# Splitting the attention output weights on GpSimd, and the last token tile in column pieces

## The chip, the cores and the metric

The kernel runs on one core of a Trainium2 chip. The metric is device microseconds of one execution, the median of several runs. A core has a matmul engine (TensorE, PE in the views, with its weight loads shown apart as PEld), an engine for elementwise work on two inputs (VectorE, DVE), one for functions of one input (ScalarE, ACT), a general engine (GpSimd, POOL) and a queue that issues transfers (SyncE, SP).

## The reference

One layer of a diffusion backbone: 1024 latent tokens and 256 context tokens, 1024 features, everything in float32.

```python
h_x = _modulate(x, g_pre_mix[l], sh1, sc1)
u_x, q_x, k_x, v_x = _project(h_x, w_in[l])
attn_x = _neighbourhood_attention(q_x, k_x, v_x, k_c, v_c, rpb[l])   # 8 heads of 64, 8 x 16 window + context keys
mix_x = jnp.concatenate([_pool_mixer(u_x, ...), attn_x], axis=-1) @ w_out[l]
x = x + gt1 * _rmsnorm(mix_x, g_post_mix[l])
y_x = _sq_relu_mlp(_modulate(x, g_pre_mlp[l], sh2, sc2), w_mlp_in[l], w_mlp_out[l])   # 1024 -> 4096 -> 1024
x = x + gt2 * _rmsnorm(y_x, g_post_mlp[l])
```

The change touches two places: the preparation of `w_out` while the attention runs, and the end of the second MLP matmul with the last norm and the residual sum.

## The kernel before

A float32 operand of a large matmul is written as a sum of two parts, `hi` (the value rounded to the matmul's short float32 format, type `F32R`) and `lo` (what is left). A product is then three matmuls: hi by hi, hi by lo, lo by hi (`three`, lines 167 to 170). So each weight tile has to be split once before use: a rounding copy for `hi` and a subtraction of two tiles in SBUF for `lo`.

**Attention** (lines 641 to 854). The work is cut into 32 units: 4 pairs of heads by 8 bands of 128 tokens. A loop over `i` runs as a pipeline written out by hand: for unit `i` the scores (`scores`, PE matmuls `S`, line 669, then one DVE instruction per head that adds a bias table and takes the minimum, line 683), the exponentials (`exps`, ACT, line 692); for unit `i - 1` the reciprocals of the sums (`share`, DVE: `RECIPROCAL` line 696, then a `COPY` that spreads them over 128 columns, `rb`, line 698); for unit `i - 2` the transposes (`turn`, PE, line 711: first `rb`, into `pa` and `pz`, then the probabilities, into `T`) and the copies of their results (lines 725 and 730); for unit `i - 3` the products with the values (`values`, PE, `pa`, line 745), and for unit `i - 4` the weighting (`weighed`, DVE, line 755). PE, ACT, DVE and SP keep the order of the program in this loop (`in_order`); GpSimd does not, there a planner in the compiler sets the order.

Two kinds of side work lie in the loop. After each group of 8 units the group's result is split for the output projection (`mixed_split`, a copy on ACT, line 766, and a subtraction on DVE, line 767, 128x512 each, named `mix`). And the first 512 output columns of `w_out`, four tiles `raw_o[0, kk]` of 128x1024 that are loaded at `i` in `LOADS`, are split in eight halves of 128x512, at `i` in `HALVES`: again a copy on ACT (`wo_..h`, line 766) and a subtraction on DVE (`wo_..l`, line 767). GpSimd meanwhile only makes the bias tables (`tables`, line 613, 12 instructions of 128x128 for each pair of heads). The first matmuls that use the split weights come after the scores of the last unit (`out_sums`, `po`).

**The end** (lines 1212 to 1321). The second MLP matmul is computed in a scheme of seven block products P1 to P7, each for four token tiles `t` of 128 tokens and 512 columns. The last products are P3 into `z` (upper 512 columns of tiles 0 to 3) and P4 into `v` (lower 512 columns of tiles 4 to 7, after P7 and the first half of P4 were summed there). For each tile the last sums are 12 matmuls (`z`) or 24 (`v`) of 128x512, and then `finish` runs:

- `c`, DVE, line 1263: the PSUM result plus `u2`, 128x512;
- the residual of the tile before (`end`: `xo`, DVE, line 1255, then its store on SP's queue, line 1256);
- `gated`: the mean square of `c` (ACT, line 130, tile `jy`, with an instruction that reads out the accumulator) and `row`, `c` times the gate (DVE, line 1246);
- `vy` (DVE, line 137) adds the mean squares of the two halves, and `ry` (GpSimd, line 139) takes the power -1/2.

Tile 7 is the last one. Its residual is done in two pieces of 512 columns, each followed by its store.

Of the kernel before, what the change touches and what calls it, by code (L numbers as in the profile page):

```python
# [10 lines left out]
F32 = mybir.dt.float32  # L11
F32R = mybir.dt.float32r
# [5 lines left out]
P = 128  # L18
D = 1024
# [60 lines left out]
def hybrid_block(ctx, tc, x, ctx_in, w_mod, b_mod, gp1, gp2, w_in, pool_w, rpb, w_out, w1, w2, vectors,  # L80
                 mask, edge, out):
    nc = tc.nc
    sub, mul, add = ALU.subtract, ALU.mult, ALU.add
# [3 lines left out]
    whl = ctx.enter_context(tc.tile_pool(name="whl", bufs=8))  # L87
# [7 lines left out]
    def sm(name, n, bufs=1):  # L95
        return small.tile([P, n], F32, tag=name.split("_")[0], name=name, bufs=bufs)
# [5 lines left out]
    @contextmanager  # L102
    def in_order(*engines):
        block = nc.cur_bb
        n = len(block.bb.instructions)
        last = {}
        yield last
        assert nc.cur_bb is block
        for i in block.bb.instructions[n:]:
            if i.engine in engines:  # L110
                if i.engine in last:
                    tc.add_manual_dep(i, last[i.engine].name,
                                      mybir.DependencyInfo(mybir.DependencyClass.NoSync, mybir.DependencyReason.DATA),
                                      reason="order")
                last[i.engine] = i
# [13 lines left out]
    def mean_square(junk, src, ms):  # L129
        nc.scalar.activation(junk, src, AF.Square, scale=D ** -0.5, accum_out=ms)  # L130

    def rsqrt_of(name, ms, more=None):
        v = sm(f"v{name}", 1, 4)
        if more is None:
            nc.vector.tensor_scalar_add(v, ms, EPS)
        else:
            nc.vector.scalar_tensor_tensor(v, ms, EPS, more, add, add)  # L137
        r = sm(f"r{name}", 1, 4)
        nc.gpsimd.tensor_tensor(r, v, nhalf, ALU.pow)  # L139
        return r  # L140
# [26 lines left out]
    def three(ps, ahi, alo, bhi, blo, first, last, more=False):  # L167
        nc.tensor.matmul(ps, ahi, bhi, start=first, stop=False, skip_group_check=more)  # L168
        nc.tensor.matmul(ps, ahi, blo, start=False, stop=False, skip_group_check=more)  # L169
        nc.tensor.matmul(ps, alo, bhi, start=False, stop=last, skip_group_check=more)  # L170
# [46 lines left out]
    def lasting(name):  # L217
        return ps_t.tile([P, 512], F32, tag="T", name=name)
# [4 lines left out]
    with tc.tile_pool(name="ps1", bufs=6, space=PSUM) as ps1, tc.tile_pool(name="tmp1", bufs=3) as tmp:  # L223

        def bank(name):
            if name[:2] == "pm" or name in ("pxt0_6", "pxt0_7", "pxt1_6", "pxt1_7", "pct2", "pct3"):
                return lasting(name)
            return ps1.tile([P, 512], F32, tag="mm", name=name)
# [7 lines left out]
        last = startup.enter_context(in_order(ET.PE, ET.Activation, ET.DVE, ET.SP))  # L236
# [192 lines left out]
        for k in range(KT):  # L429
            for i in range(2):  # L430
                o = (k % 2) * 256 + i * P
                nc.tensor.transpose(pct[k // 2][:, o : o + P], cp[i][:, k * P : (k + 1) * P], ident)
        hc = []
        for k in range(KT):
            if k % 2 == 0:
                hp = page(f"hc{k}", F32R)
            o = (k % 2) * 512
# [9 lines left out]
        rest, closing = [], []  # L447
# [49 lines left out]
        for i in range(2):  # L497
            ps = bank(f"pkc{i}")
# [8 lines left out]
        for i in range(2):  # L507
            ps = bank(f"pvc{i}")
# [11 lines left out]
        for m in range(NM):  # L520
            ps = bank(f"pv{m}")
# [59 lines left out]
        for g in range(4):  # L581
            up = page(f"u{g}")
            for b in range(2):
                ps = bank(f"pu{g}_{b}")
# [56 lines left out]
    with (  # L641
# [4 lines left out]
        bank = lasting  # L646
# [112 lines left out]

        kks = (2, 3, 0, 1)  # L760
        raw_o, wo = {}, {}
        LOADS, HALVES = (8, 10, 17, 19), (12, 13, 14, 20, 21, 22, 28, 30)
        lows = []

        def high(src, hi, lo):
            nc.scalar.copy(hi, src)
            lows.append(lambda: nc.vector.tensor_tensor(lo, src, hi.bitcast(F32), sub))
# [6 lines left out]
            mp = mix[b][4 + j] = page(f"mix{b}_{4 + j}", F32R)  # L774
            high(mixed[j, b], mp[:, :512], mp[:, 512:])

        def weight_split(n):
            kk, cs = kks[n // 2], slice(n % 2 * 512, n % 2 * 512 + 512)
            if n % 2 == 0:
                wo[kk] = [whl.tile([P, 1024], F32R, tag="hl", name=f"wo0_{kk}{x}") for x in "hl"]  # L780
            hi, lo = wo[kk]
            high(raw_o[0, kk][:, cs], hi[:, cs], lo[:, cs])

        def weight_load(h, kk):
            raw_o[h, kk] = page(f"wor{h}_{kk}")
# [21 lines left out]
        with in_order(ET.PE, ET.Activation, ET.DVE, ET.SP):  # L807
            queries(1, 1, bank("pq1_1"), 0)
            for i in range(N + 4):
                if i < N and units[i][1] == 2 and units[i][0] < 3:  # L810
                    tables(units[i][0] + 1)
                if i in LOADS:
                    weight_load(0, kks[LOADS.index(i)])
                if i == N - 2:
                    G1 = gate_page("a")
                if i > 3:
                    weighed(i - 4)
                low()
                if i > 8 and i % 8 == 7:
                    mixed_split(i // 8 - 1, 1)  # L820
                if i > 0 and i % 8 == 0:
                    mixed_split(i // 8 - 1, 0)
                if i in HALVES:
                    weight_split(HALVES.index(i))
                if i < N:
                    scores(i)
                else:

                    if i == N:
                        po = ps_s.tile([P, 1024], F32, tag="S", name="po")[:, :512]  # L830
                    out_sums(po, wo, 0, ((0, 1), (2, 3, 4), (5, 6, 7), ())[i - N])
                if 1 < i <= N + 1:
                    turn(i - 2)
                    fifth_kept(i - 2)
                if i < N:
                    exps(i, 0)
                if 1 < i <= N + 1:
                    turn_kept(i - 2, 0, nc.scalar.copy)
                if i < N:
                    exps(i, 1)  # L840
                if 1 < i <= N + 1:
                    turn_kept(i - 2, 1, nc.vector.tensor_copy)
                if i < 2:
                    queries(2 + i, 1, bank(f"pq{2 + i}_1"), 0)
                if 0 < i <= N:
                    share(i - 1)
                if 2 < i <= N + 2:
                    values(i - 3)
            mixed_split(3, 1)
            low()  # L850
            out_kept(0, 0, po, page("jo0_0")[:, :512])
            po = bank("po1")
            out_sums(po, wo, 1, range(8))
            out_kept(0, 1, po, page("jo0_1")[:, :512])

    with tc.tile_pool(name="ps2", bufs=6, space=PSUM) as ps2:
# [6 lines left out]
      with ExitStack() as tmp2:  # L863
        tmp = tmp2.enter_context(tc.tile_pool(name="tmp2", bufs=4))
# [74 lines left out]
        for t in out_group(1, range(NT)):  # L939
            rs = rsqrt_of(f"m_{t}", ssm[0][:, t : t + 1], ssm[1][:, t : t + 1])  # L940
            xt = page(f"xr{t}")
# [16 lines left out]
        NG = NPAIR // 2  # L958
# [218 lines left out]
        made = {}  # L1177
# [29 lines left out]
        with tc.issue_after(first[ET.PE]), in_order(ET.PE, ET.Activation, ET.DVE, ET.SP):  # L1207
# [5 lines left out]
            tmp = tmp2.enter_context(tc.tile_pool(name="tmp3", bufs=4))  # L1213
# [5 lines left out]
                both = [page(f"{name}{i}") for i in range(2)]  # L1219
                return [both[t // 2][:, (t % 2) * 512 : (t % 2) * 512 + 512] for t in range(4)]  # L1220

            def token_sums(ps, t, groups, first, last, more):
                n = 2 * len(groups)
                for j in range(n):
                    a, w = groups[j // 2]
                    o = (j % 2) * 512
                    three(ps[t], a[0][:, o + t * P : o + (t + 1) * P], a[1][:, o + t * P : o + (t + 1) * P],
                          w[0][:, o : o + 512], w[1][:, o : o + 512], first and j == 0, last and j == n - 1, more=more)

            def group(ps, name, g, more=False):  # L1230
                prepare()
# [5 lines left out]
            sq = [sm(f"sy{h}", NT) for h in range(2)]  # L1237
            rows = {}
# [10 lines left out]
            ending = []  # L1249

            def end():
                for m, rs, xt, cuts in ending:
                    for c in range(cuts):
                        cs = slice(c * D // cuts, (c + 1) * D // cuts)
                        nc.vector.scalar_tensor_tensor(xt[:, cs], rows[m][:, cs], rs, xt[:, cs], mul, add)
                        nc.sync.dma_start(og[m][:, :, cs], xt[:, cs])
                ending.clear()

            def finish(m, h, src, xt, cuts):
                if m > 5:  # L1260
                    end()
                c = tmp.tile([P, 512], F32, tag="t", name=f"c{m}", bufs=3)
                nc.vector.tensor_tensor(c, src, u2[m % 4], add)
                end()
                gated(m, h, c)
                ending.append((m, rsqrt_of(f"y_{m}", sq[0][:, m : m + 1], sq[1][:, m : m + 1]), xt, cuts))

            x = four("pyx")
            for g in range(NG):
                group(x, "P1", g)  # L1270
                if g == 4:
                    G2 = gate_page("b")
# [4 lines left out]
            for g in range(NG):  # L1277
                group(y, "P6", g)
                if g == NG - 1:
                    u2 = halves("u2")  # L1280
# [6 lines left out]
            v, z = four("pyv"), four("pyz")  # L1287
# [10 lines left out]
            for g in range(NG // 2):  # L1298
                group(v, "P4", g, more=True)
                group(z, "P3", g, more=True)  # L1300
                c = half(4 + g, 1)
# [6 lines left out]
            xts = {}  # L1308
# [5 lines left out]
                nc.sync.dma_start(xts[m], x1d[m])  # L1314
            for t in range(4):
                token_sums(z, t, [made["P3", g] for g in (NG - 2, NG - 1)], False, True, True)
                finish(t, 1, z[t], xts[t], 1)
            for t in range(4):
                token_sums(v, t, [made["P4", g] for g in range(NG // 2, NG)], False, True, True)
                finish(4 + t, 0, v[t], xts[4 + t], 1 + (t == 3))  # L1320
            end()


# [28 lines left out]
```

## Time and profile before

| | us |
|---|---|
| median of 3 runs | 1063.97 (1063.96 to 1064.71) |
| the profiled execution | 1063.25 |
| its span, first to last instruction | 1061.5 |

| engine | busy us | share of the span | instructions |
|---|---|---|---|
| PE | 1045.0 | 98% | 5873 |
| DVE | 685.6 | 65% | 1072 |
| ACT | 506.8 | 48% | 881 |
| POOL | 55.7 | 5% | 109 |

Shares are means over stages with different limits, and consecutive matmuls overlap in the records, so a busy PE is not a PE at its peak. The chain of waits (the work that ended last, followed back from the end) tells which engine sets the time in which stage. The mean granted TensorE clock is 0.997. Views used: the page, the chain in stretches of time, the groups of instructions, single lines of the program with minimum, median and maximum of their durations, and the timeline.

### The profile page before, as it was taken

What the parts mean: (1) busy time and instruction counts of PE and PEld (TensorE: products, weight loads), DVE (VectorE), ACT (ScalarE), POOL (GpSimd) and SP (SyncE); (2) the same over time, 40 slices, a digit from 0 to 9 for tenths busy, and PEclk for the clock granted to TensorE, in tenths of its full rate; (3) what the DMA queues carried; (4) which work ended last, traced back from release to release, by engine and by line L of the source; (5) the groups of instructions that cost most, each with busy time, mean ns of one, the idle gap of its engine ahead of it and who ended that gap; (6) DMA issues with size and microseconds to landing.
All of it is one profiled execution on the core that took longest, in us unless ns stands there. A gap on an engine that the chain in (4) does not pass through costs nothing.

```text
span 1061.5 us, 15251 instructions
## 1 busy us (share of the span) xinstructions
PE 1045.0 (98%) x5873; PEld 856.4 (81%) x5873; DVE 685.6 (65%) x1072; ACT 506.8 (48%) x881; POOL 55.7 (5%) x109
## 2 busy tenths in 40 slices
PE   7999999999999999999999999999999999999996
PEld 6788888867888888888888888888888888888885
DVE  6436634855999235799986666665577566557586
ACT  7554121235998123876555455554553335334441
POOL 2020000040120002200000000000000000000001
PEclk9999999999999999999999999999999999999998
DMA  9905740441111605445845445345597666546556
GB/s 343 324 21 198 243 174 0 138 134 40 42 41 47 174 1 171 145 149 183 259 168 175 140 138 190 129 151 196 209 355 253 243 238 220 192 164 205 173 188 206
DMA packets 94268, 179.37 MB, mean 169 GB/s; under 512 B 6898, under 2 KB 39154, under 8 KB 94196
## 3 DMA queue, kind: packets, MB, share of 16 engines
q1 hardware_dynamic: 76644, 144.80, 41.6%
q10 hardware_dynamic: 16272, 29.40, 7.5%
q0 software_dynamic: 1280, 4.21, 1.1%
q8 instruction: 46, 0.75, 0.3%
q14 instruction: 26, 0.21, 0.1%
HBM read 140.62 MB, written 37.76 MB: 168 GB/s over the span
## 4 chain that ended last, share of the span: by engine, by line
PE 89%; ACT 3%; DVE 3%; DMA 2%; SPq 1%; issue 1%; POOL 1%; POOLq 0%; DVEq 0%; ACTq 0%
PE pk L382 4%; PE S L669 3%; PE pa L745 3%; PE pyv L169 3%; PE pyv L168 3%; PE pyz L169 3%; PE pyz L168 3%; PE pyx L169 3%; PE phv L170 3%; PE phz L170 3%; PE pyx L170 3%; PE phz L168 3%; PE phv L168 3%; PE phv L169 3%; PE phz L169 3%; PE pyx L168 3%
## 5 line engine op out<-in xcount | busy, mean ns | idle before, releaser
L1001 ACT ACTIVATE c<-c 128x512 f32<-128x512 f32 x48 | 30.3, 632 | 60.4 <-DVE c L1114 23.8
L692 ACT ACTIVATE sp<-sp,nm 128x640 f32<-128x640 f32 (+1 forms) x64 | 51.3, 802 | 8.4 <-DVE nm L683 7.8
L683 DVE CUSTOM_DVE_ANT_0 sp<-S,tab 128x640 f32<-128x640 f32 (+1 forms) x56 | 42.8, 802 | 16.5 <-PE S L669 9.4
L144 DVE TENSOR_TENSOR wpS<-S,wpS 128x512 fp32r<-128x512 f32 x64 | 43.6, 686 | 11.8 <-ACT wpS L143 11.8
L168 PE MATMUL phx<-thB,wpA 128*128 128x512 f32 x128 | 49.9, 390 | 0.0
L170 PE MATMUL phx<-thB,wpA 128*128 128x512 f32 x128 | 49.9, 390 | 0.0
L169 PE MATMUL phx<-tlB,wpA 128*128 128x512 f32 x128 | 49.8, 389 | 0.0
L143 ACT CAST wpS<-S 128x512 fp32r<-128x512 f32 x64 | 39.2, 616 | 17.9 <-PE phy L170 7.5
L139 POOL TENSOR_TENSOR ry<-vy,nhalf 128x1 f32<-128x1 f32 x8 | 4.4, 550 | 600.7 <-DVE vy L137 600.7
L1002 ACT ACTIVATE c<-c 128x512 f32<-128x512 f32 x48 | 30.3, 631 | 8.0 <-DVE sa L1072 7.4
L1108 DVE TENSOR_TENSOR c<-phz,u 128x512 f32<-128x512 f32 x16 | 11.1, 691 | 32.2 <-PE phz L170 32.1
L669 PE MATMUL S<-kT,q 64*128 64x384 f32 (+1 forms) x128 | 27.9, 495 | 0.4 <-DVE nm L683 0.4
L170 PEld LDWEIGHTS phx<-thB,wpA 128*128 128x128 f32 x128 | 24.0, 188 | 5.2 <-DVE wpA L144 0.2
L169 PEld LDWEIGHTS phx<-tlB,wpA 128*128 128x128 f32 x128 | 24.0, 188 | 5.0
L168 PEld LDWEIGHTS phx<-thB,wpA 128*128 128x128 f32 x128 | 24.0, 188 | 4.9
L805 DVE TENSOR_TENSOR mp<-pw,Ga 128x512 f32<-128x512 f32 x14 | 9.6, 688 | 27.5 <-ACT jo L130 27.5
L745 PE MATMUL pa<-pt,v 128*64 128x128 f32 x352 | 25.9, 279 | 1.0 <-ACT px L725 0.3
L168 PE MATMUL phy<-thT,wpS 128*128 128x512 f32 x64 | 24.9, 389 | 0.0
L169 PE MATMUL phy<-tlT,wpS 128*128 128x512 f32 x64 | 24.9, 389 | 0.0
L170 PE MATMUL phy<-thT,wpS 128*128 128x512 f32 x64 | 24.9, 389 | 0.0
L168 PE MATMUL phz<-thT,wpS 128*128 128x512 f32 x64 | 24.9, 389 | 0.0
L169 PE MATMUL phz<-tlT,wpS 128*128 128x512 f32 x64 | 24.9, 389 | 0.0
(924 smaller groups left out, 3267.5 us busy)
## 6 DMA issues: line engine op xcount, KB each, us to landing
b<-in_w SPq DMA_DIRECT2D x64, 512.0 KB, 4.6
hrS<-hdS SPq DMA_DIRECT2D x32, 512.0 KB, 4.7
hrA<-hdA SPq DMA_DIRECT2D x24, 512.0 KB, 5.2
wm<-in_w_mod SPq DMA_DIRECT2D x16, 512.0 KB, 9.6
wa_0w<-in_w SPq DMA_DIRECT2D x16, 512.0 KB, 5.2
wa_1w<-in_w SPq DMA_DIRECT2D x16, 512.0 KB, 4.1
hdA<-c ACTq DMA_DIRECT2D x32, 256.0 KB, 2.3
hdS<-sa ACTq DMA_DIRECT2D x32, 256.0 KB, 4.3
```

The source lines that it names most:

```text
L143: nc.scalar.copy(hi, src)
L144: nc.vector.tensor_tensor(lo, src, hi.bitcast(F32), sub)
L168: nc.tensor.matmul(ps, ahi, bhi, start=first, stop=False, skip_group_check=more)
L169: nc.tensor.matmul(ps, ahi, blo, start=False, stop=False, skip_group_check=more)
L170: nc.tensor.matmul(ps, alo, bhi, start=False, stop=last, skip_group_check=more)
L382: nc.tensor.matmul(pks[b][j], wk(wgt, k, low, j * P, P), r, start=(k == 0 and n == 0), stop=(k == KT - 1 and n == 2))
L669: nc.tensor.matmul(S[e][:, c0 : c0 + keys.shape[1]], q[hs, cols], keys[hs], start=True, stop=True)
L683: nc.vector.tensor_tensor_reduce(out=to, in0=s, in1=bt, scale=1.0, scalar=BIG, op0=add, op1=ALU.min, accum_out=nm)
L692: nc.scalar.activation(sp, sp, AF.Exp, bias=least[i, e], scale=-1.0, accum_out=sums[i][:, e : e + 1])
L745: nc.tensor.matmul(pa[e * HD : (e + 1) * HD, cols], v[:, f : f + HD], turns[i][:, e, c] if c < 4 else fifths[i][:, :, (e + 1) * HD : (e + ...
L1001: nc.scalar.activation(r, src, AF.Relu)
L1002: nc.scalar.activation(r, r, AF.Square)
```

## The change

First, `w_out`'s tiles are split by GpSimd, one whole 128x1024 tile at a time, at `i` = 11, 13, 21 and 23, with a copy and a subtraction, and ACT's and DVE's sixteen instructions for the halves are gone. `mixed_split` stays on ACT and DVE.

Second, tile 7's lower 512 columns are made in two pieces of 256. Before the last four tiles, `late` adds up the upper 256 of these columns as they stand in PSUM and `u2`, on DVE. Then 24 matmuls of 128x256 complete the first piece, 24 more compute the second piece's last part alone in another PSUM bank, and each piece has its own `c`, mean square and `row` (`finish_last`). One more small addition on DVE joins the mean squares. The residual and its store are done in three pieces, of 512, 256 and 256 columns.

```diff
-        LOADS, HALVES = (8, 10, 17, 19), (12, 13, 14, 20, 21, 22, 28, 30)
+        LOADS, SPLITS = (8, 10, 17, 19), (11, 13, 21, 23)
...
-        def weight_split(n):
-            kk, cs = kks[n // 2], slice(n % 2 * 512, n % 2 * 512 + 512)
-            if n % 2 == 0:
-                wo[kk] = [whl.tile([P, 1024], F32R, tag="hl", name=f"wo0_{kk}{x}") for x in "hl"]
-            hi, lo = wo[kk]
-            high(raw_o[0, kk][:, cs], hi[:, cs], lo[:, cs])
+        def weight_split(kk):
+            hi, lo = wo[kk] = [whl.tile([P, 1024], F32R, tag="hl", name=f"wo0_{kk}{x}") for x in "hl"]
+            nc.gpsimd.tensor_copy(hi, raw_o[0, kk])
+            nc.gpsimd.tensor_tensor(lo, raw_o[0, kk], hi.bitcast(F32), sub)
...
-                if i in HALVES:
-                    weight_split(HALVES.index(i))
+                if i in SPLITS:
+                    weight_split(kks[SPLITS.index(i)])
...
-            def token_sums(ps, t, groups, first, last, more):
+            def token_sums(ps, t, groups, first, last, more, c0=0, nc0=512):
...
+                    ws = slice(o + c0, o + c0 + nc0)
                     three(ps[t], a[0][:, o + t * P : o + (t + 1) * P], a[1][:, o + t * P : o + (t + 1) * P],
-                          w[0][:, o : o + 512], w[1][:, o : o + 512], first and j == 0, last and j == n - 1, more=more)
+                          w[0][:, ws], w[1][:, ws], first and j == 0, last and j == n - 1, more=more)
...
-                    for c in range(cuts):
-                        cs = slice(c * D // cuts, (c + 1) * D // cuts)
+                    for c0, c1 in zip(cuts, cuts[1:]):
+                        cs = slice(c0, c1)
...
+            def finish_last(m, pieces, xt):
+                end()
+                so = sm("so", 1)
+                for c0, src, more in pieces:
+                    cs = slice(c0, c0 + 256)
+                    c = tmp.tile([P, 512], F32, tag="t", name=f"c{m}_{c0}", bufs=3)[:, :256]
+                    nc.vector.tensor_tensor(c, src, more, add)
+                    jk = tmp.tile([P, 512], F32, tag="t", name=f"jy{m}_{c0}", bufs=3)[:, :256]
+                    s0 = sq[0][:, m : m + 1]
+                    mean_square(jk, c, s0 if c0 else so)
+                    nc.vector.tensor_tensor(rows[m][:, cs], c, G2[:, cs], mul)
+                    if c0 == 0:
+                        nc.vector.tensor_tensor(so, so, sq[1][:, m : m + 1], add)
+                ending.append((m, rsqrt_of(f"y_{m}", s0, so), xt, (0, 512, 768, 1024)))
...
-            for t in range(4):
-                token_sums(v, t, [made["P4", g] for g in range(NG // 2, NG)], False, True, True)
-                finish(4 + t, 0, v[t], xts[4 + t], 1 + (t == 3))
+            late = u2[3][:, 256:]
+            nc.vector.tensor_tensor(late, v[3][:, 256:], late, add)
+            groups = [made["P4", g] for g in range(NG // 2, NG)]
+            for t in range(3):
+                token_sums(v, t, groups, False, True, True)
+                finish(4 + t, 0, v[t], xts[4 + t])
+            v[3] = v[3][:, :256]
+            token_sums(v, 3, groups, False, True, True, 0, 256)
+            rest = {3: bank("pye_0")[:, :256]}
+            token_sums(rest, 3, groups, True, True, False, 256, 256)
+            finish_last(7, ((0, v[3], u2[3][:, :256]), (256, rest[3], late)), xts[7])
             end()
```

More of the change, by code (lines that the diff above doesn't have):

```diff
@@ L1257, in end, with finish @@
                 ending.clear()
-            def finish(m, h, src, xt, cuts):
+            def finish_last(m, pieces, xt):
[12 more added lines that the diff above has]
+                ending.append((m, rsqrt_of(f"y_{m}", s0, so), xt, (0, 512, 768, 1024)))
+            def finish(m, h, src, xt):
                 if m > 5:
@@ L1265, in finish @@
                 gated(m, h, c)
-                ending.append((m, rsqrt_of(f"y_{m}", sq[0][:, m : m + 1], sq[1][:, m : m + 1]), xt, cuts))
+                ending.append((m, rsqrt_of(f"y_{m}", sq[0][:, m : m + 1], sq[1][:, m : m + 1]), xt, (0, D)))
             x = four("pyx")
@@ L1316, in hybrid_block @@
                 token_sums(z, t, [made["P3", g] for g in (NG - 2, NG - 1)], False, True, True)
-                finish(t, 1, z[t], xts[t], 1)
-            for t in range(4):
-                token_sums(v, t, [made["P4", g] for g in range(NG // 2, NG)], False, True, True)
-                finish(4 + t, 0, v[t], xts[4 + t], 1 + (t == 3))
+                finish(t, 1, z[t], xts[t])
+            late = u2[3][:, 256:]
[9 more added lines that the diff above has]
+            finish_last(7, ((0, v[3], u2[3][:, :256]), (256, rest[3], late)), xts[7])
             end()
```

## The prediction

> **What bounds the kernel now.** I read the page first, for the engines' shares and the chain.
>
> ```profile
> span 1061.5 us, 15251 instructions
> PE 1045.0 (98%) x5873; PEld 856.4 (81%) x5873; DVE 685.6 (65%) x1072; ACT 506.8 (48%) x881; POOL 55.7 (5%) x109
> PE 89%; ACT 3%; DVE 3%; DMA 2%; SPq 1%; issue 1%; POOL 1%; POOLq 0%; DVEq 0%; ACTq 0%
> ```
>
> PE carries 89% of the chain, so taking work from ACT or DVE is worth only what those engines hold on the chain in that stage. GpSimd is nearly idle. Next, the chain in two stretches of the attention: an inner unit without a weight half, then units 11 and 12, then the other places where a weight half lies on the chain.
>
> ```profile
> 258.45 1.28 PE S L669 x8
> 259.90 0.50 PE T L711 x16
> 260.41 1.24 PE pa L745 x20
> 261.65 0.52 PE S L669
> ```
> ```profile
> 276.79 1.42 PE S L669 x8
> ...
> 281.24 0.51 ACT wo_2h L766
> ...
> 282.02 1.31 PE pa L745 x20
> 283.33 0.84 PE S L669 x3
> ...
> 306.46 0.51 ACT wo_3h L766
> 312.57 0.60 DVE wo_0l L767
> 338.22 0.51 ACT wo_1h L766
> ```
>
> Columns are start, length, what. A unit without side work goes from scores to scores in 261.65 - 258.45 = 3.20 us, all of it PE. Units 11 and 12 take 283.33 - 276.79 = 6.54 us, 0.14 more than twice 3.20, although 0.51 us of a weight half lies on their chain: PE's own path runs just behind. Last, the chain at the end.
>
> ```profile
> 1053.14 0.24 PE pyv L170
> ...
> 1053.40 0.70 DVE c L1263
> ...
> 1054.18 0.63 ACT jy L130
> ...
> 1054.94 0.17 DVE vy L137
> ...
> 1055.22 0.59 POOLq L1348
> ...
> 1055.83 0.75 DVE xo L1255
> ```
>
> Here every step waits for the one before. The POOLq piece covers the reciprocal root on GpSimd.
>
> **Part 1, what leaves ACT and DVE.** Sixteen instructions of 128x512 go. Only four are on the chain: 0.51 + 0.51 + 0.60 + 0.51 = 2.13 us, the most that can come back. Where the next path can be read, one such place cost 0.14, and four are 0.56. I take 0.9, nearer to the second, because it is the row that shows both paths. What is late next is PE itself. The first use of the split weights comes after unit 31's scores, so that GpSimd needs long for them costs nothing there.
>
> **Part 1, what goes to GpSimd.** No copy or subtraction of 128x1024 on GpSimd is in the trace; these rows are nearest.
>
> ```profile
> L185 POOL MEMSET accsc<- 128x1024 f32 x1 | 1.0, 975 | 0.0
> 265.42 5.12 POOL L613 TENSOR_TENSOR tab<-msk,U 128x128 f32<-128x128 f32 x12 [30.69 <-DMA U<-in_rpb]
> ```
>
> The copy: not under the memset's 0.98 us; I take 1.0. The subtraction: one of 128 columns takes 5.12 / 12 = 0.427 us, eight times that is 3.4, and the memset's 0.98 is the other end. I take 2.4, nearer to the row of the same operation; an assumed 0.13 or so of the 0.427 will not grow with the columns (0.3 x 8 = 2.4). The Trainium skill (GPSIMD Engine Reference, section 3.1) measured 4497 ns for an addition of 2048 columns, so an estimate of 2.25 us here; no run here shows it yet, and the sum by it would be 0.3 us lower.
>
> What matters is what these hold up. Views of single lines (minimum/median/maximum) and the timeline around 296 us, where GpSimd makes tables:
>
> ```profile
> L698 DVE COPY rb<-ri x32: 226/227/333, 245.3 to 346.8; 128x128 f32<-128x128 f32 x32
> L767 DVE TENSOR_TENSOR mix<-f,mix x8: 679/682/750, 271.3 to 355.8; 128x512 fp32r<-128x512 f32 x8
> L613 POOL TENSOR_TENSOR tab<-msk,U x48: 437/452/907, 221.4 to 299.7; 128x128 f32<-128x128 f32 x48
> ```
> ```profile
> 296.00 0.46 POOL L613 TENSOR_TENSOR tab<-msk,U 128x128 f32<-128x128 f32 x1
> 296.20 0.33 DVE L698 COPY rb<-ri 128x128 f32<-128x128 f32 x1
> 296.66 0.75 DVE L767 TENSOR_TENSOR mix<-f,mix 128x512 fp32r<-128x512 f32 x1
> 296.81 0.91 POOL L613 TENSOR_TENSOR tab<-msk,U 128x128 f32<-128x128 f32 x1
> ```
>
> The `COPY` that normally takes 0.227 us starts inside a GpSimd operation, takes 0.333 and ends 0.07 us after it. The subtraction `mix`, which reads two tiles in SBUF, is 0.07 longer, and the GpSimd operation that begins beside it takes 0.907 instead of 0.452. One side waits until the other is through. With 0.45 us operations this costs a tenth; with 2.4 us ones the same wait can be 2.4. The Trainium skill says so (SBUF — State Buffer, section "SBUF: two separate sides"): VectorE and GpSimd share a port pair as an exclusive lock held for a whole instruction, against VectorE operations in a two-port mode or with two SBUF inputs. The rows agree, with 0.33 against 0.227.
>
> The `COPY rb` comes once in every 3.20 us. Its slack:
>
> ```profile
> 258.84 0.23 DVE L698 COPY rb<-ri 128x128 f32<-128x128 f32 x1
> ```
>
> It ends at 259.07. The transposes that read it are next on PE behind scores that last until 258.45 + 1.28 = 259.73, so 0.66 us of wait is free and the rest stops PE; queued behind it on DVE are `weighed` and the next scores' minimum, which PE also needs. For a `COPY` at a random moment of the period, a hold of h costs on the mean (h - 0.66)² / (2 x 3.20): 0.47 for 2.4, 0.02 for 1.0. Four pairs: 4 x 0.49 = 2.0 us. The ends: nothing, if each pair falls into the gap between two `COPY`s (1.0 + 2.4 is 0.2 more than a period, so a small wait remains, within the slack), and 4 x (2.4 - 0.66) = 7.0, if each subtraction begins just ahead of one.
>
> **Part 2, the end.** PE: 24 matmuls of 512 columns, 0.227 us apart (1053.14 is the last), become 48 of 256, each with its own weight load. If the pitch halves, nothing changes. If the load sets it:
>
> ```profile
> 112.56 1.84 PE L204 MATMUL pcsh<-ones,accsh 128*128 128x1 f32 x16
> L170 PEld LDWEIGHTS phx<-thB,wpA 128*128 128x128 f32 x128 | 24.0, 188 | 5.2 <-DVE wpA L144 0.2
> ```
>
> Sixteen loads with matmuls of one column take 1.84 us, 0.115 each: 48 x 0.115 = 5.52 against 24 x 0.227 = 5.45, so +0.1. (A load's record is 0.188 long, but loads that follow each other at 0.115 overlap.)
>
> After the last matmul the path has 256 columns in `c` and in the mean square. The columns' prices:
>
> ```profile
> L755 DVE TENSOR_TENSOR f<-pa,px 128x128 f32<-128x128 f32 x32 | 9.1, 284 | 3.9 <-PE pa L745 3.9
> L130 ACT ACTIVATE mp<-xr 128x1024 f32<-128x1024 f32 x8 | 8.5, 1062 | 16.1 <-DVE xr L943 16.1
> ```
>
> `c`: 0.70 at 512 and 0.284 at 128 columns are 1.08 ns a column, so 256 fewer save 0.28. The mean square: 1.062 at 1024 and 0.63 at 512 are 0.84 ns, so 0.21. Together -0.49. The first piece's `c`, `row`, mean square and the extra addition run while PE makes the second: half of 5.45, 2.7 us, hides them. `late`, about 0.42 us on DVE, needs idle time there two tiles earlier:
>
> ```profile
> 1042.52 0.69 DVE L1263 TENSOR_TENSOR c<-pyv,u 128x512 f32<-128x512 f32 x1 [0.58 <-PE pyv L170]
> ```
>
> DVE waits 0.58 us for PE before tile 5, which covers it; without that cover it would cost 0.42.
>
> The stores:
>
> ```profile
> 1056.61 1.20 SPq L1256 DMA_DIRECT2D out<-xo  x2
> out<-xo SPq DMA_DIRECT2D x1, 512.0 KB, 3.7
> out<-xo SPq DMA_DIRECT2D x2, 256.0 KB, 2.9
> ```
>
> Two issues take 1.20 us, some 0.66 from one to the next with the wait between them. The third piece's issue is thus 0.66 behind where the second's was: SP's queue sets it, not DVE, whose pieces get shorter. Its transfer is shorter: 3.7 us for 512 KB and 2.9 for 256 leave between 2.5 (along the line) and 2.9 (a fixed cost) for 128 KB. So +0.26 to +0.66, taken at +0.4. The end as a whole: +0.1 - 0.49 + 0.4 = 0.0, from -0.2 to +0.3; the third piece gives back what the half columns save. I count +0.1, for the extra addition's wait.
>
> **The sum.** -0.9 + 2.0 + 0.1 = +1.2 us. The profiled execution took 1063.25 (span 1061.5 and 1.75 around it), so 1064.45 for one like it; it is 0.72 under the median of 1063.97, against which the forecast is 1065.2 us. A measurement of this kernel can tell about 0.2%, 2.1 us, from no change; +1.2 is inside.
>
> **The rivals.**
>
> *GpSimd stops DVE nearly every time* (slower). A pair starts when its tile has landed or the tables are done, moments tied to the loop's own rhythm, so the phase need not be random. If three of four subtractions begin just ahead of a `COPY`, or one ahead of a `mix` subtraction, the loss is 3 x 1.74 = 5.2 and more, and the sum +3 to +6: 1067 to 1070. For it: 1.0 + 2.4 us of GpSimd work cannot miss a `COPY` in 3.20. Against it: the one that meets the 1.0 us copy's end waits little. It decides from the point where the waits exceed 0.66 us by more than 3.0 in total (the 0.9 gained and 2.1). Chance 0.29.
>
> *The waits stay in the slack* (faster). The pairs sit well or the subtraction is near 1 us; then -0.6 to -2.1 with the end at 0: 1061.9 to 1063.4. Chance 0.16, a bit under half of it faster by over 0.2%.
>
> *The narrow matmuls are bound by their weight loads in full*: 48 x 0.188 = 9.0 against 5.45, +3.6, about 1068.7. Against it stand the 16 loads in 1.84 us. Chance 0.05.
>
> **How the numbers follow.** My forecast (waits in part beyond the slack, from -0.6 to +2.1) has 0.50, all within 0.2%. Slower by over 0.2%: 0.29 + 0.05 = 0.34. Faster by over 0.2%: 0.07. Within: 0.50 + 0.09 = 0.59. The range that holds 8 in 10 leaves out the best of the second rival and the worst of the first: 1062.3 to 1068.4 us.
>
> **What would show it.** Right: `rb` copies and `mix` subtractions much over 0.227 and 0.68 us wherever GpSimd's new operations run, PE idle in `turn` behind them, inner units elsewhere at 3.20, no `wo` on the chain, 48 matmuls about 0.114 apart, the last store issued over 2 us after the reciprocal root. Wrong: `rb` unchanged beside long GpSimd operations (then there is no lock), GpSimd's subtraction near 1 or over 3 us, units still over 3.20 without a wait for DVE (the gain was not there), or a pitch of 0.19 at the end.

## The result: 4.6 us slower, and the profile after

| | before | after |
|---|---|---|
| median, us | 1063.97 (6 runs) | 1068.58 (6 runs, 1066.78 to 1070.59) |
| the profiled execution, us | 1063.25 | 1068.69 |
| its span, us | 1061.5 | 1066.9 |

The ratio is 1.0043, interval [1.0031, 1.0054]: slower by more than the 0.2% that can be told apart, 3.4 us more than the forecast and 0.2 us above the end of its range.

The page of after: span, engines, and the shares of the chain of waits.

```profile
span 1066.9 us, 15309 instructions
PE 1049.1 (98%) x5897; PEld 860.5 (81%) x5897; DVE 687.9 (64%) x1069; ACT 503.9 (47%) x875; POOL 69.6 (7%) x117
PE 90%; DVE 4%; ACT 2%; issue 1%; DMA 1%; POOL 1%; SPq 0%; POOLq 0%; DVEq 0%; ACTq 0%
```

GpSimd is busy 13.9 us longer and has 8 instructions more, as the diff says. DVE has 3 instructions fewer but is busy 2.3 us longer: some of its instructions became longer. The views of single lines (minimum/median/maximum) tell which:

```profile
L698 DVE COPY rb<-ri x32: 226/227/2280, 245.5 to 352.1; 128x128 f32<-128x128 f32 x32
L767 DVE TENSOR_TENSOR mix<-f,mix x8: 679/682/2786, 275.1 to 361.1; 128x512 fp32r<-128x512 f32 x8
```

The medians stand at 227 and 682 ns; the maxima went from 333 to 2280 and from 750 to 2786. The timeline of after shows where (GpSimd's first two pairs, then DVE beside them):

```profile
251.76 1.04 POOL L779 CAST wo_2h<-wor 128x1024 fp32r<-128x1024 f32 x1 [16.66 <-DMA wor<-in_w_out]
252.88 2.34 POOL L780 TENSOR_TENSOR wo_2l<-wor,wo_2h 128x1024 fp32r<-128x1024 f32 x1
273.88 1.05 POOL L779 CAST wo_3h<-wor 128x1024 fp32r<-128x1024 f32 x1
275.01 2.36 POOL L780 TENSOR_TENSOR wo_3l<-wor,wo_3h 128x1024 fp32r<-128x1024 f32 x1
```
```profile
253.02 2.28 DVE L698 COPY rb<-ri 128x128 f32<-128x128 f32 x1
255.22 0.81 DVE L683 CUSTOM_DVE_ANT_0 sp<-S,tab 128x640 f32<-128x640 f32 x1
274.76 0.25 DVE L698 COPY rb<-ri 128x128 f32<-128x128 f32 x1
275.13 2.79 DVE L767 TENSOR_TENSOR mix<-f,mix 128x512 fp32r<-128x512 f32 x1
```

GpSimd's first subtraction began 0.14 us ahead of an `rb` copy, the second 0.12 us ahead of a `mix` subtraction. Both DVE instructions got no further while GpSimd's ran: it ended at 252.88 + 2.34 = 255.22 and `rb` 0.08 later; the second ended at 275.01 + 2.36 = 277.37 and `mix` 0.55 later, most of the 0.68 that it needs by itself. The first pair is written at `i` = 11, but the planner put it where its tile landed, during unit 3: GpSimd had waited 16.66 us for the transfer.

What followed on PE is in the chain of waits, around unit 3 and around units 9 and 10 (start, length, what):

```profile
253.02 2.29 DVE rb L698
255.31 0.14 issue
255.44 0.34 PE pa L711
...
256.03 0.85 PE T L711 x16
256.88 1.86 PE pa L745 x16
...
260.20 0.50 PE T L711 x16
```
```profile
275.21 2.71 DVE mix L767
277.92 0.73 DVE sp L683
...
278.71 2.09 PE S L669 x7
```

After the `rb` of 2.29 us PE's own work is slow too: 16 transposes take 0.85 us, one unit later 0.50. The busy times by stretch say why (behind the length of the stretch stand PE, PEld, DVE, ACT and POOL, each with its number of instructions, then the granted clock):

```profile
253.40:255.40 2.00, 0.31 (x2) 0.00 (x0) 2.00 (x2) 0.41 (x2) 1.82 (x1) 0.94 0.00 0
255.40:258.70 3.30, 3.25 (x40) 2.88 (x40) 2.38 (x7) 2.65 (x7) 0.00 (x0) 0.52 0.02 5
258.70:261.90 3.20, 3.20 (x54) 2.61 (x52) 2.14 (x6) 1.46 (x5) 0.00 (x0) 1.00 0.00 0
```

PE stood for 1.74 us (from 253.71 to 255.45) and then ran at half clock for 3.4 us. Before has no such stretch in the loop.

From the start of each unit's scores to the next, in us (all other units differ by 0.02 at most, or cancel with their neighbour):

| unit | before | after | difference |
|---|---|---|---|
| 3 | 3.72 | 7.05 | +3.33 |
| 7 | 3.02 | 3.29 | +0.27 |
| 9 to 12 | 12.47 | 14.02 | +1.55 |
| 18 to 20 | 9.40 | 9.63 | +0.23 |
| 27, 28, 30 | 10.42 | 10.09 | -0.33 |

They make +5.05 of the 5.4 us between the two spans; against the median of before the profiled execution of after is 4.7 longer. In units 12, 20, 27, 28 and 30, where a weight half lay, the gain is there; it is outweighed by the waits. Not all of these are beside the new operations: the `rb` that costs 0.27 in unit 7 (0.50 us, at 268.74) is held by an operation of the tables, which before has too.

At the end, the chain of after:

```profile
1058.92 0.13 PE pye L170
...
1059.08 0.43 DVE c L1265
...
1059.60 0.42 ACT jy L130
...
1060.14 0.17 DVE vy L137
...
1060.42 0.59 POOLq L1372
```
```profile
1061.81 1.83 SPq L1255 DMA_DIRECT2D out<-xo  x3
```

From the last matmul's end to the end of the span there are 7.81 us, 8.11 before. The 48 narrow matmuls are 0.120 us apart (5.76 us for what took 5.45), so the end comes out even.

### The profile page after: what moved, and what is told of

Read it like the earlier page. It is cut to its first block, busy times and chain, and to the rows that moved or that the text cites. A ratio compares the mean times of both kernels' runs of the same rounds, so it can differ in the third digit from the quotient of the medians.

```text
span 1066.9 us, 15309 instructions
## 1 busy us (share of the span) xinstructions
PE 1049.1 (98%) x5897; PEld 860.5 (81%) x5897; DVE 687.9 (64%) x1069; ACT 503.9 (47%) x875; POOL 69.6 (7%) x117
## 4 chain that ended last, share of the span: by engine, by line
PE 90%; DVE 4%; ACT 2%; issue 1%; DMA 1%; POOL 1%; SPq 0%; POOLq 0%; DVEq 0%; ACTq 0%
PE pk L382 4%; PE S L669 3%; PE pa L745 3%; PE pyz L170 3%; PE pyz L169 3%; PE pyx L170 3%; PE phv L168 3%; PE phz L168 3%; PE pyx L168 3%; PE phz L169 3%; PE phv L169 3%; PE phv L170 3%; PE phz L170 3%; PE pyx L169 3%; PE pyz L168 3%; PE pyv L170 3%
```

## The experiments

The theory: GpSimd's long operation holds up a DVE instruction that begins beside it (`rb`, `mix`); that stops PE; and a pause of some 2 us brings half clock on top. The rivals: the end costs the time; the work on GpSimd costs it without any wait; a wait costs only its length.

**The two parts apart.** e1 has the attention part alone, e2 the end alone.

```diff
 e1, against before
-        LOADS, HALVES = (8, 10, 17, 19), (12, 13, 14, 20, 21, 22, 28, 30)
+        LOADS, SPLITS = (8, 10, 17, 19), (11, 13, 21, 23)
...
 e2, against before
+            finish_last(7, ((0, v[3], u2[3][:, :256]), (256, rest[3], late)), xts[7])
...
```

> Attention part of the change alone, the end as before. Theory (a wait of DVE behind GpSimd's long operations, made longer by a halved TensorE clock after the PE stall): all of the loss is here, 1068.4 us, between 1066.7 and 1070.5 as in the changed kernel's own runs, with one rb copy near 2.3 us and one mix subtraction near 2.8. Rival (the narrow matmuls and third store at the end carry part of it): 1 us or more below the changed kernel in the median.

> End part alone, the weights split on ACT and DVE as before. Theory: PE +0.3 (48 matmuls 0.120 apart for 24 at 0.227), half columns -0.5, third store +0.25: 1064.0 us, not to be told from before (1063.97). Rival (end slower): 1064.5 or more.

e1: 1069.48 us, 1.0057 [1.0044, 1.0069]. e2: 1063.76 us, 0.9998 [0.9989, 1.0007]. The whole loss is the attention's, and the end is worth nothing that can be measured. In e1 the same two instructions are held (`rb` 2.406 us at 253.41, `mix` 2.787 at 277.04), and half clock follows both, for 6.8 and 3.4 us. (The traced execution is the longest of e1's five, 1072.02 us, so this is its worst case.)

**The same work on GpSimd in short pieces.**

```diff
-            nc.gpsimd.tensor_copy(hi, raw_o[0, kk])
-            nc.gpsimd.tensor_tensor(lo, raw_o[0, kk], hi.bitcast(F32), sub)
+            for c0 in range(0, 1024, 128):
+                cs = slice(c0, c0 + 128)
+                nc.gpsimd.tensor_copy(hi[:, cs], raw_o[0, kk][:, cs])
+                nc.gpsimd.tensor_tensor(lo[:, cs], raw_o[0, kk][:, cs], hi[:, cs].bitcast(F32), sub)
```

> Attention part alone, but GpSimd splits each tile in eight pieces of 128 columns (copy, subtraction, copy, ...), so that no operation lasts over 0.5 us; same columns in all. Theory (an exclusive wait for one whole GpSimd operation): every rb copy waits at most 0.45 us, inside its slack of 0.66, PE never stalls long enough for a lower clock, the weights' absence from ACT and DVE is kept: 1063.1 us, 1062.5 to 1063.8. Rival (GpSimd's work beside DVE costs by its amount, not by the length of one operation): as slow as the attention part in whole tiles, 1066 or more.

1063.69 us, 0.9999 [0.9990, 1.0008]: 5.8 us less than e1 for GpSimd work on the weights that is longer in total (21.6 us beside 13.6 in the traces). The single lines of e3:

```profile
L698 DVE COPY rb<-ri x32: 226/227/575, 246.0 to 347.7; 128x128 f32<-128x128 f32 x32
L767 DVE TENSOR_TENSOR mix<-f,mix x8: 680/688/923, 272.7 to 356.7; 128x512 fp32r<-128x512 f32 x8
```

A waiting DVE instruction gets in between two GpSimd operations (the longest `rb` is 0.35 over its 0.227, and a subtraction of 128 columns takes 0.46 to 0.51), so the length of one operation is what counts, not the work. Unit 3 is back at 3.72. The forecast for e3 was 0.6 lower: waits of some 0.3 us still cost +0.28, +0.33 and +0.29 in units 7, 10 and 18, where there is next to no slack. The one in unit 7 is again beside an operation of the tables.

**The same work, but `rb` on another engine.**

```diff
-            nc.vector.tensor_copy(shares[i].rearrange("p (e t) -> p e t", e=2),
+            nc.scalar.copy(shares[i].rearrange("p (e t) -> p e t", e=2),
```

> Attention part alone, and the rb copy is made by ACT (which has its own way to SBUF, if the theory holds) in place of DVE. Theory: no rb copy waits, units 3 and 18 go back to about 3.7 and 2.9 us, unit 3's halved clock is gone; only mix subtractions that meet a whole-tile operation still wait (up to 2.1 us once), and ACT carries 0.2 us more a unit: 1063.5 to 1066.0 us. Rival (the stall comes from GpSimd's traffic, whoever copies): 1067 or more.

1071.78 us, 1.0070 [1.0058, 1.0083], above the expected range and where the rival put it. The single lines are still the theory's and not the rival's: `rb` is no longer held, but escaping the lock this way bought nothing. The single lines of e4:

```profile
L698 ACT COPY rb<-ri x32: 281/286/302, 250.1 to 355.4; 128x128 f32<-128x128 f32 x32
L767 DVE TENSOR_TENSOR mix<-f,mix x8: 681/685/2795, 273.2 to 364.4; 128x512 fp32r<-128x512 f32 x8
```

On ACT no `rb` is over 0.302 us, although GpSimd's operations are as long as in after, and unit 3 takes 4.28; `mix`, which stayed on DVE, is still held. What took the gain away is in e4's trace. Units 9 to 12, with the held `mix` and a stretch at half clock behind it, are 3.9 us longer than in before; the other units are 4.3 us longer in sum, and there ACT is now on the chain: inner units take 3.32 to 3.57 us in place of 3.20.

The rows are from the chain of e4 at 290 to 300 us.

```profile
294.29 0.53 ACT px L725 x2
294.81 0.82 ACT sp L692 x2
295.64 0.48 ACT pt L730
```

**A pause without GpSimd.** The kernel before, with plain additions on DVE ahead of the `rb` of unit 1, the instruction that was held: 2.4 us of them in e5; the same in e6, where PE is given 18 transposes to do meanwhile; 1.3 us of them in e10.

```diff
+            if i == 1:
+                dm = att.tile([P, 512], F32, tag="dm", name="dm")
+                for n in (512, 512, 512, 256):            # e10: (512, 512)
+                    nc.vector.tensor_tensor(dm[:, :n], vcp[:, :n], vcp[:, 512 : 512 + n], add)
...
+                if i == 3:                                # e6 alone
+                    for _ in range(18):
+                        nc.tensor.transpose(pz[:, 256:384], ident, ident)
```

> The kernel before, with nothing moved to GpSimd; DVE does 2.1 us of extra additions ahead of the rb copy of unit 1, where the changed kernel's copy waited 2.05 us. Theory (the stall is dear because a PE idle for 2 us comes back at half the clock for 3.4 us): unit 3 grows from 3.72 to about 7.1 us, by some 1.2 more than the stall, a stretch of 3.4 us at clock 0.5 begins near 255 us, and the time is 1067.3 us. Rival (PE is slowed by GpSimd's reads beside it): no lower clock, unit 3 at 5.8 us, 1066.0 us.

> The same stall, with 18 transposes of a constant on PE between unit 3's scores and unit 1's transposes, that is, in the time in which PE would stand idle. Theory: PE is not idle, the clock stays at 1.0, unit 3 takes 5.8 to 5.9 us and the time is 1066.0 us, over 1 us less than with the idle PE. Rival (the lower clock follows from DVE's stall or by chance): the half clock shows here too, 1067.3 us.

> The kernel before, with two extra VectorE additions of 128x512 (about 0.6 us each, so 1.2 us) in front of the rb copy of unit 1 and nothing on GpSimd: a shorter pause of PE than in e5, at the same place. Theory (a short pause costs its length, and the half clock comes only after a pause of some 2 us): unit 3 takes about 4.9 us in place of 3.7, no half clock in the loop, 1064.0 + 1.2 = 1065.2 (1064.8 to 1065.6). Rival (any pause at this place brings 3.4 us at half clock): 1.2 + 1.3 to 1.7 more, 1066.5 to 1066.9.

e5: 1068.71 us, 1.0043 [1.0029, 1.0057]. e6: 1066.22, 1.0020 [1.0011, 1.0029]. e10: 1064.92, 1.0011 [1.0001, 1.0020]. Stretches with the granted clock of e5, e6 and e10, in this order (of e5 and e6 the pause first):

```profile
254.16:256.20 2.04, 0.00 (x1) 0.01 (x1) 1.97 (x5) 0.11 (x2) 0.00 (x0) 1.00 0.00 0
257.00:260.40 3.40, 3.40 (x25) 2.42 (x22) 1.76 (x6) 2.28 (x6) 0.00 (x0) 0.50 0.02 5
```
```profile
253.70:255.80 2.10, 2.10 (x20) 1.93 (x22) 2.03 (x5) 0.09 (x1) 0.00 (x0) 1.00 0.00 0
255.80:262.00 6.20, 6.20 (x98) 5.02 (x100) 5.07 (x16) 5.30 (x14) 0.00 (x0) 1.00 0.02 4
```
```profile
254.70:258.70 4.00, 3.99 (x72) 3.34 (x74) 3.21 (x11) 3.19 (x9) 0.00 (x0) 1.00 0.02 4
```

In e5 PE stands for 2.06 us and then runs 3.4 us at half clock; units 3 and 4 are 3.87 longer. In e6 PE is as late for its own work (within 0.05 us, counted from the first scores) but not idle: no half clock, unit 3 is 2.27 longer. The difference of 1.60 is the clock's. In e10 PE stands for 0.87 us, the clock stays, and unit 3 is 1.09 longer. So here the short pause costs about its length and the long one 1.6 us more; a pause on DVE alone, without GpSimd, is enough for both. e5's forecast was 1.4 too low: the additions took 2.43 us and not 2.1, the clock's part was 1.6 and not 1.2, and what makes up the rest is open.

**One pair moved.** The whole change; the first pair's copy and subtraction each wait for an `rb` copy, so that they begin just behind it.

```diff
+            c = nc.gpsimd.tensor_copy(hi, raw_o[0, kk])
+            if kk == 2:
+                tc.add_manual_dep(getattr(c, "ins", c), getattr(rb_copy[3], "ins", rb_copy[3]).name,
...
+            d = nc.gpsimd.tensor_tensor(lo, raw_o[0, kk], hi.bitcast(F32), sub)
+            if kk == 2:
+                tc.add_manual_dep(getattr(d, "ins", d), getattr(rb_copy[4], "ins", rb_copy[4]).name,
...
```

> The whole change, but the copy and the subtraction of the first of the four weight tiles wait for the rb copies of units 3 and 4; the other three tiles run as in the change. Theory (of the change's 4.6 us, 3.3 are the first pair's: 2.05 us of waiting and 1.3 at half clock): unit 3 falls back to 3.7, the waits of units 9, 10 and 18 stay, about 1.8 and 0.5 us: 1068.6 - 3.3 = 1065.3 (1064.6 to 1066.3; the phase of the later pairs may shift by the change in unit lengths). Rival (the loop's rhythm pulls the stall to another unit, so that one pair less frees nothing): 1067.5 to 1068.6.

1065.00 us, 1.0012 [1.0003, 1.0021]: 3.6 us less than the change, for the moment at which two instructions begin. In its profiled execution (1066.65, the longest of its eleven) unit 3 is back at 3.72. The second pair is where it was, and its `mix` is held as before:

```profile
L768 DVE TENSOR_TENSOR mix<-f,mix x8: 681/682/2782, 272.2 to 358.6; 128x512 fp32r<-128x512 f32 x8
```

Units 9 and 10 take 4.40 and 3.61. PE stood for 1.25 us there, and no half clock followed. Units 14 and 19 are 0.52 and 0.40 longer than in before: there the third and the fourth pair hold an `rb`, 1.06 and 0.63 us long.

**All pairs moved.** e7 has the attention part alone, e8 the whole change; the copy waits for the last `rb` ahead of it in the program and the subtraction for the next one, at `i` = 11, 13, 19 and 21 (the change has 21 and 23 for the last two).

```diff
+        def behind_rb(ins):
+            tc.add_manual_dep(getattr(ins, "ins", ins), getattr(rb_copy[-1], "ins", rb_copy[-1]).name,
...
+            behind_rb(nc.gpsimd.tensor_copy(hi, raw_o[0, kk]))
...
+            behind_rb(nc.gpsimd.tensor_tensor(lo, raw_o[0, kk], hi.bitcast(F32), sub))
...
+                    weight_high(kks[SPLITS.index(i)])
+                if i - 1 in SPLITS:
+                    weight_low(kks[SPLITS.index(i - 1)])
```

> Attention part alone, whole tiles on GpSimd, but each of its operations is made to wait for an rb copy: the copy of a tile behind the one in the unit before (at 11, 13, 19, 21), the subtraction behind the next one. Theory: an operation of 1.04 or 2.36 us that begins right behind one rb copy is over before the next (3.2 us later), and at these places no mix subtraction is due; rb stays at 0.23 us save beside tables, no PE stall over 0.3, no lower clock in the loop, the 0.9 us is kept: 1063.1 us. Rival (length and amount of GpSimd's work cost, not where it begins): 1066 or more, as in the attention part alone.

> The whole change with the same waits for GpSimd. Theory: as the kernel with the waits alone and the end part's 0.1 to 0.3 less: 1062.9 us, faster than before by about 0.1%. Rival: 1066 or more.

e7: 1063.16 us, 0.9992 [0.9983, 1.0001]. e8: 1063.00 us, 0.9990 [0.9981, 1.0000]. e7's GpSimd timeline and e8's single lines:

```profile
281.61 2.37 POOL L789 TENSOR_TENSOR wo_2l<-wor,wo_2h 128x1024 fp32r<-128x1024 f32 x1 [1.87 <-DVE rb L699]
287.96 2.37 POOL L789 TENSOR_TENSOR wo_3l<-wor,wo_3h 128x1024 fp32r<-128x1024 f32 x1 [2.21 <-DVE rb L699]
```
```profile
L699 DVE COPY rb<-ri x32: 226/227/326, 245.5 to 346.4; 128x128 f32<-128x128 f32 x32
L768 DVE TENSOR_TENSOR mix<-f,mix x8: 681/682/751, 271.5 to 355.4; 128x512 fp32r<-128x512 f32 x8
```

The same operations, just as long (2.37 us), hold up nothing: begun behind an `rb`, they are over before the next one, 3.20 us later. The waits also move the pairs to other units (the first from unit 3 to units 11 and 12); that another place without the wait would have done as much is not excluded. In e8 units 12, 20 and 28 take 3.20, and first to last scores 104.00 us, 104.72 before. e8 has the lowest median of all kernels here. Its distance from before, 1.0 us, is at the edge of what can be told.

**The third store.** e8 with the last tile's residual in two parts.

```diff
-                ending.append((m, rsqrt_of(f"y_{m}", s0, so), xt, (0, 512, 768, 1024)))
+                ending.append((m, rsqrt_of(f"y_{m}", s0, so), xt, (0, 512, 1024)))
```

> The whole change with GpSimd's operations each made to wait for an rb copy (as in e8), and the last tile's residual in two parts, columns 0 to 512 and 512 to 1024, in place of three. In the run with three parts the last store was issued 4.0 us after PE's last matmul and landed 2.5 us later (128 KB); with two parts the second store goes out when the second of three stores did in time, about 3.6 (3.40 plus some 0.2 for a ry of 512 columns), and carries 256 KB, which took 2.87 us in the kernel before: 6.3 to 6.5 against 6.55. Expected 0.0 to 0.25 us less than e8, 1062.85 (1062.5 to 1063.2). If the third store costs what the prediction priced it at (0.26 to 0.66 us) the time is 1062.4 to 1062.75.

1063.09 us, 0.9992 [0.9983, 1.0001]: no difference from e8 in the medians. In the traces the part from the last matmul's end to the end of the span is 7.62 us, 7.81 with three parts, so the third store costs some 0.2 (e2, with three parts too, has 7.91). The medians can't show that.

## Why the prediction was wrong

**What leaves ACT and DVE, -0.9: right.** e8, without the waits, has 0.72 us less between first and last scores, and its median is 1.0 under before; e7, without the end part, is 0.9 under it.

**GpSimd's durations, 1.0 and 2.4: right.** 1.03 to 1.05 and 2.34 to 2.37 us were measured. The estimate of 2.25 from the Trainium skill (GPSIMD Engine Reference, section 3.1) was 0.1 low; it would not have changed the outcome.

**The lock: right.** `rb` and `mix` waited for GpSimd to end, and were 2.28 and 2.79 us long. This agrees with the Trainium skill (SBUF — State Buffer, section "SBUF: two separate sides"): the shared pair of ports is held for a whole instruction, against VectorE operations in a two-port mode or with two SBUF inputs.

**What the waits cost, +2.0: the step that failed.** The loop of after is 5.05 us longer than before's, and without the waits it would be 0.72 shorter (e8): 5.8 us in all, 0.27 of it beside the tables. Four things in that step were off:

- *The random phase.* The prediction took the mean over a uniform phase, 0.49 for each pair. The pairs start at moments that the loop and the transfers set, and two of four subtractions began 0.14 and 0.12 us ahead of the instruction that they held, in e1 0.03 and 0.12. The second of these is not a random phase: in after, e1, e4 and e11 alike the second pair's subtraction began 0.11 to 0.13 us ahead of a `mix`. In three of them it began just as the `rb` ahead of that `mix` ended, which the tile's copy on GpSimd had held (in after at 275.01, 274.76 + 0.25); in e4, with `rb` on ACT, it did so without this. The rival "GpSimd stops DVE nearly every time" had this mechanism and the time, 1067 to 1070, with a chance of 0.29; of its two conditions the second came, one subtraction just ahead of a `mix`, and one ahead of a `COPY` beside it. e11 shows the weight of one such meeting: 3.6 us.
- *The `mix` subtractions.* The sum priced waits of the `COPY` alone. A held `mix`, whose first signs the prediction had in its rows, stood only in the rival. One of them made units 9 to 12 longer by 1.55 us, and by 1.80 in e11, where it is the only long hold there.
- *The slack.* 0.66 us was read in an inner unit and used for all. Unit 3 stands where DVE is on the chain already: there 2.43 us of additions cost 2.27 (e6) and 1.29 cost 1.09 (e10), a slack of 0.2. In unit 7 an `rb` of 0.50 cost 0.27, all that it was longer; the next one, 0.51 long at 271.47, cost nothing. The slack has to be read place by place.
- *The price of a stop.* (h - 0.66) counted the wait alone. In after unit 3 lost 3.33 us to a hold of 2.05; by e6's slack of 0.2 some 1.9 of it is the wait and 1.4 the half clock behind it (1.60 in e5 against e6). No row of before showed that, since PE never stands that long in its loop.

**The end, 0.0: right in sum, its terms off.** `c` and the mean square gave -0.48 (predicted -0.49: `vy` ends 1.26 us after the last matmul, 1.74 before). The narrow matmuls cost +0.3, three times the +0.1, since their pitch is 0.120 and not 0.115. The third store cost about +0.2 and not +0.4. The extra addition in `late` shows no cost.

**What was to show it.** `rb` and `mix` much over 0.227 and 0.682, PE idle in `turn`, inner units at 3.20 or 3.21, no `wo` on the chain, the last store issued 2.09 us after the reciprocal root: all seen. The pitch at the end was 0.120 and not 0.114. The sign that was missing from the list is the granted clock.

## What to carry to other kernels

Moving work to an idle engine is priced by the length of one operation there and by what begins beside it, not by the engine's idle share: cut it into pieces shorter than the slack (e3, -5.8 us), or tie its start to just behind the instruction that it would hold up (e7, -6.3). Where two engines run in a fixed rhythm, don't take a mean over their phase; go through the places one by one, with the slack of each. And price a stop of PE of about 2 us with what the clock can add.

## What was not expected of the hardware

Not every DVE instruction waits. Beside GpSimd's third subtraction (293.49 to 295.86 us) the timeline of after has:

```profile
293.92 0.82 DVE L683 CUSTOM_DVE_ANT_0 sp<-S,tab 128x640 f32<-128x640 f32 x1
294.67 0.69 DVE L730 COPY pt<-T 128x512 f32<-128x512 f32 x1
295.27 0.15 DVE L696 RECIPROCAL ri<-su 128x2 f32<-128x2 f32 x1
295.46 0.49 DVE L698 COPY rb<-ri 128x128 f32<-128x128 f32 x1
```

The instruction with one operand in PSUM, the copy out of PSUM and the reciprocal take their usual time; only the copy within SBUF ends with GpSimd's operation.

The clock went to half for 3.4 us after PE had stood for 1.74 (after) and 2.06 us (e5), and for 6.8 after 1.86 (e1). After 0.87 (e10), 1.00 (after, units 9 and 10) and 1.25 (e11) it did not; after 1.26 in e1 and 0.84 with 0.35 in e4 it did. The traces' record of the clock shows that the length of the pause alone doesn't decide it. In every trace the changes of the clock lie whole multiples of 3.41 us apart (in e1 half from 255.26 to 262.09, full for 20.48, half again from 282.57), and in e5 the half clock began 0.77 us after PE had resumed. So it counts how a pause lies to these stretches. In the loop PE had stood for at least 1.06 us (e4) within the stretch ahead of each change to half clock, and for at most 1.04 (e11) within those that none followed. But at the end of the kernel, in after, it stood for 1.66 us within one and the next was at full clock. What sets the limit is open. The Trainium skill (TensorE: Matmul & The Clock Gate, Part 1 and "Why this matters for your kernels") has the half rate come after an idle window of about 3.4 us and warns of pauses over some 3 us; here shorter ones were enough, and the stretches were as long as its window, or twice as long.

After's six executions lie between 1066.78 us at a mean clock of 0.998 and 1070.59 at 0.993. That the same waits bring half clock more or less often would fit this, but only one of the six was traced, so it is not shown.
